# First stage of a hybrid decoder block: norm weights spread by TensorE, ten input slots, another order of loads

## The chip, the cores and the metric

The kernel runs on one core of one Trainium2 chip. The metric is the device time of one execution in microseconds (us). A core has TensorE (PE; its weight loads are listed as PEld), VectorE (DVE), ScalarE (ACT), GpSimd (POOL) and SyncE (SP). Each of them runs its own instructions in program order and waits for the others at semaphores. In this stage SP issues all the DMA transfers.

## What is computed

One decoder block in float32 on x (1024 tokens by 1024 channels) with 256 memory tokens. The first stage computes the three lines below; everything else (gates, state space, forgetting attention, output, cross-attention, FFN) comes after it.

```
u = rms_norm(h, norm_mix[l])
proj = u @ w_in[l]            # the first 512 columns are u_ssm
...
k, v = jnp.split(m @ w_kv, 2, axis=-1)     # m = rms_norm(mem, norm_mem_kv)
```

The state-space branch then needs, for 32 groups of 16 channels with 64 complex states each, lam_bar = exp(lam dt), b_bar = (lam_bar - 1) / lam * b, c and d_skip:

```
bu = jnp.einsum('gpn,blgn->blgp', b_bar, uf)
_, states = lax.associative_scan(...)      # state = lam_bar * state + bu
y = jnp.einsum('gnp,blgp->blgn', c, states).real + d_skip * uf
```

## The kernel before

A float32 product is made of three matmuls on a high and a low part of both operands (`mm3`, L168 to L170: hi*hi, lo*hi, hi*lo). Every operand is split by `split`: ACT casts the high part (L178), then DVE, or POOL where the order says so, subtracts it for the low part (L179). A weight tile is loaded into one of two slots `raw` and split into one of four slots `whi` and `wlo`; a load waits until the tile two before it has been split, and a split waits until the GEMM that used its slot last is through.

**First stage** (`stage_in`). Its work is written as steps, and the table `ORDER_IN` gives their order: F fetches a tile of 128 tokens (m and n are the memory, 0 to 7 are x), G fetches the norm weights, Q, R and S square, take the root and scale a tile (L360, L193 to L203, L217), T turns half a tile by four transposes on PE (L223), E casts and splits the turned half (`uh`, `ul`; `mh`, `ml` for the memory), D loads a weight tile and W splits it (D0 to D7 are the memory's keys and values, D8, D9, Da, Db four blocks of 128 columns of w_in), K and V are the GEMMs of the memory, and U is a GEMM for 128 channels (first digit) and 512 tokens (second digit) with 24 matmuls of 512 columns. X warms PE up. L loads the parameters of the state space (`S5.load`), P are the pieces of `S5.prepare`. A scheduler places the steps' instructions on each engine by the order of the table and by when it believes them ready; a queue then runs as placed. The GEMMs U stand in the order U00 U10 U20 U21 U11 U30 U31 U01, before and after. Where later steps need a slot of `whi`, it is therefore the one of Da's block that comes free first (after U21), then D9's (U11), Db's (U31) and last D8's, after U01, the last GEMM of the stage.

**Parameters.** `S5.load` fetches lam, log_dt, c (in eight transfers), b and d_skip, then turns lam, log_dt and c on PE into `par` and `cT`. `S5.prepare`, all on DVE, makes the powers of lam_bar: exponentials (`exp_parts`, L248 to L257), sine and cosine (`sincos`, L270 to L288, tiles `trg_...`, two of them in the slots that the fetched c leaves), the tables `la` and `ld` (L1205, L1208), and the input coefficients `bb_re`, `bb_im` (L1232 to L1237).

**Second stage** (`stage_ssm`). 32 gate GEMMs of 24 matmuls of 512 columns run on PE. Between them, for each of four quarters q: `weights(q)` on POOL and DVE builds `fre` and `fim` (L1279 to L1282), `Gm` (L1290 to L1298) and the rotations `EC` and `ES` by seven doublings (L1311 to L1313, five on POOL, two on DVE); `turn_weights` turns `fre` and `fim` on PE (L1330) and multiplies them with c (`misc`, L1336), before gate 4 + 7q; `states` reads the stored u (`xg`, L1354), multiplies it with the turned weights (L1361, before gate 5 + 7q) and runs the scan on DVE and POOL (L1369 to L1390); `out` is before gate 9 + 7q. The tiles `fre`, `fim` and their products have one slot each, so `weights(1)` writes `fre` once PE has read the one of quarter 0.

Of the kernel before, what the change touches and what calls it, by code (L numbers as in the profile page):

```python
# [9 lines left out]
F32 = mybir.dt.float32  # L10
# [9 lines left out]
P = 128  # L20
D = 1024
L = 1024
# [16 lines left out]
RSLOT_LATE = (0, 1, 2, 3, 4, 4, 5, 5, 6, 6, 7, 7)  # L39

ORDER_IN = """
G0 Fm Qm Fn D1 X24 Qn Rm D0 Sm F1 G1 Tm0 Rn Em0 Sn Tn0 F0 Tm1 W0 Q0 Tn1 En0 F2 Q1 W1g En1 Em1 K0 D2 F3 K1 R0
S0 T00 T01 k0 E00 Q2 W2g D3 E01 D4 S1 T10 Q3 W3 k1 D5 K3 K2 W4 E10 W5 D6 R1 k2 T11 k3 S2 F4 Q4 V0 F5 S3g T30
E11 D7 Q5 F7 T20 R2 T21 E21 E20 S4 E30 W6 W7 T40 V1 D8 S5 E40 W8 T31 V2 L0 T41 E31 V3 D9 Db T50 F6 Q6 v T51 W9
E51 U00 Da Q7 L1 E41 u00 R3 S6 Wa T60 E50 S7 T61 T70 Wbg E61 U10 E60 P0 U20 u10 T71 E70 E71 u20 P1 U21 U11 U30
P2 u30 U31 u11 u31 U01 u21 P3 P4 P5 u01
"""


# [284 lines left out]
def stage_in(B, xp, s5, x, mem, g_mix, g_kv, w_in, w_mem_kv, uT, u_d, kv_d):  # L334

    V, A, T, S, small = B.V, B.A, B.T, B.S, B.small  # L340
    junk = xp.tile([P, D], BF16, name="junk")
    mT = Act(xp, "mT", 4, 8, ML, kg=4, name="m")
    tiles, gain, ss, rs, raw, w, ps, us, kv = {}, {}, {}, {}, {}, {}, {}, [], []
    names = {"m": -2, "n": -1, **{str(t): t for t in range(NT)}}

    def xtile(name="xt"):
        return xp.tile([P, D], F32, tag="xt", bufs=8, name=name)

    def fetch(t):
        tiles[t] = xtile()  # L350
        S.dma_start(tiles[t], mem[(t + 2) * P:(t + 3) * P, :] if t < 0 else x[t * P:(t + 1) * P, :])

    def gains(i):
        gain[i] = xtile("gain")
        S.dma_start(gain[i], (g_kv if i == 0 else g_mix).partition_broadcast(P))

    def square(t):
        if t % 2 == 0:
            ss[t // 2] = small.tile([P, 2], F32, name="ss2")
        A.activation(junk, tiles[t], AF.Square, scale=1.0 / 32, accum_out=ss[t // 2][:, t % 2:t % 2 + 1])  # L360

    def root(i):
        rs[i] = B.rsqrt(ss[-1][:, i % 2:i % 2 + 1] if i < 0 else ss[i], pool=i < 0)

    def scale(t, pool):
        i = t // 2
        r = rs[t][:, 0:1] if t < 0 else rs[i][:, t % 2:t % 2 + 1]
        B.norm_scale(tiles[t], tiles[t], r, gain[0 if t < 0 else 1], pool=pool)

    def turn(t, b):  # L370
        ps[t, b] = B.turn(tiles[t], b, ("misc", "pv")[b])

    def evac(t, b):
        B.turned(ps.pop((t, b)), b, *((mT, t + 2) if t < 0 else (uT, t)))

    def wget(i):
        if i < 4:
            src = w_mem_kv[:, i * P:(i + 1) * P]
# [5 lines left out]
        S.dma_start(raw[i].rearrange("p (k c) -> p k c", k=D // src.shape[-1]),  # L384
                    src.rearrange("(k p) c -> p k c", p=P))
# [24 lines left out]
    def values(kk):  # L410
        wh, wl = w[4 + kk]
        for t in range(2):
            if kk == 0:
                ps["v", t] = B.bank("sc")
            for k in (2 * kk, 2 * kk + 1):
                B.mm3(ps["v", t], *mT.tok(k, t), wh[:, k % 2, :], wl[:, k % 2, :], k == 0, k == 7)

    def values_out():
        for t in range(2):
            cs = slice(t * 512, (t + 1) * 512)  # L420
            B.split(kv[2][:, cs], kv[3][:, cs], ps.pop(("v", t)))
        for i in range(2, 4):
            S.dma_start(kv_d[i], f32(kv[i]))

    def ssm_in(q, h):
        ps["u", q, h] = B.bank("mm")
        B.gemm_t(ps["u", q, h], *w[8 + q], uT, h, 8)

    def ssm_out(q, h):
        if h == 0:  # L430
            us.append(xp.tile([P, D], F32, tag="kv", bufs=4, name="us"))
        uv = us[q].rearrange("p (t c) -> p t c", t=8)
        A.copy(uv[:, :, 64 * h:64 * h + 64], ps.pop(("u", q, h)).rearrange("p (c t) -> p t c", t=8))
        if h == 1:
            S.dma_start(u_d[q].rearrange("t p c -> p t c"), uv)

    prep = s5.prepare()

    acts = {"F": lambda a: fetch(names[a]), "G": lambda a: gains(int(a)), "Q": lambda a: square(names[a]),
            "R": lambda a: root(names[a]),  # L440
            "S": lambda a: scale(names[a[0]], a[1:] == "g"),
            "T": lambda a: turn(names[a[0]], int(a[1])), "E": lambda a: evac(names[a[0]], int(a[1])),
            "D": lambda a: wget(int(a, 16)), "W": lambda a: wsplit(int(a[0], 16), a[1:] == "g"),
            "K": lambda a: keys(int(a)), "k": lambda a: keys_out(int(a)), "V": lambda a: values(int(a)),
            "v": lambda a: values_out(), "U": lambda a: ssm_in(int(a[0]), int(a[1])),
            "u": lambda a: ssm_out(int(a[0]), int(a[1])), "L": lambda a: s5.load(int(a)),
            "P": lambda a: next(prep, None), "X": lambda a: B.warm(int(a))}
    for step in ORDER_IN.split():
        acts[step[0]](step[1:])
# [661 lines left out]
class S5:  # L1111
# [9 lines left out]
    def load(self, part):  # L1121
# [5 lines left out]
        def pt(name, shape, dt=F32):  # L1127
            return sp.tile([P] + shape, dt, name=name)

        if part == 0:  # L1130
# [4 lines left out]
            S.dma_start(self.ldr[32:48, :], log_dt.rearrange("(j two) -> j two", two=2))  # L1135
            self.craw = []
            for src in (c_re, c_im):
                cr = sp.tile([P, 256], F32, tag="craw", bufs=2, name="craw").rearrange("p (h q) -> p h q", h=2)
                for h in range(2):
                    for two in range(2):  # L1140
                        S.dma_start(cr[:, h, 64 * two:64 * two + 64],
                                    src.rearrange("(j two) m p -> two j m p", two=2)[two, 8 * h:8 * h + 8])
                self.craw.append(cr)
            self.braw = [pt("b_re", [16, 16]), pt("b_im", [16, 16])]
# [3 lines left out]
            S.dma_start(self.dbc, d_skip.partition_broadcast(P))  # L1148
            return
        V.tensor_copy(self.rows[32:48, :].rearrange("j (two p) -> j two p", two=2),  # L1150
                      self.ldr[32:48, :].unsqueeze(2).to_broadcast([16, 2, 64]))
        ps = B.bank("misc")
        T.transpose(ps[:, :48], self.rows, ident[0:48, 0:48])
        self.par = pt("par", [48])
        V.tensor_copy(self.par, ps[:, :48])
        self.cT = [pt("cT_re", [16, 16]), pt("cT_im", [16, 16])]
        for t_, cr in zip(self.cT, self.craw):
            ps = B.bank("misc")
            for h in range(2):
                T.transpose(ps[:, h * P:(h + 1) * P], cr[:, h, :], ident)  # L1160
            V.tensor_copy(t_, ps[:, :256].rearrange("p (j m) -> p j m", j=16))

    def prepare(self):
        B, sp, cT, bb, dbc, par = self.B, self.sp, self.cT, self.braw, self.dbc, self.par
        V, A, G = B.V, B.A, B.G
        lr, li, ld = par[:, 0:16], par[:, 16:32], par[:, 32:48]

# [73 lines left out]
        for i in range(2):  # L1241
            G.memset(self.cb[i], 0.0)
            for g in range(2):
                V.tensor_scalar(out=self.cb[i][64 * g:64 * g + 64, :, g, :], in0=cT[i][64 * g:64 * g + 64],
                                scalar1=1.0 if i == 0 else -1.0, scalar2=None, op0=ALU.mult)

        msk = pt("msk", [16])
# [563 lines left out]
```

## Time and profile before

| | |
|---|---|
| time, median of 3 runs (lowest to highest) | 1593.38 us (1593.16 to 1594.76) |
| time of the profiled execution | 1588.78 us |
| its span, first to last instruction | 1586.7 us |
| PE busy in the span | 1534.0 us (97%) |
| DVE / ACT / POOL busy | 1019.5 / 655.2 / 254.3 us |
| last matmul of the first stage (L170, U01) | 112.06 us, for 0.23 us |
| mean granted clock of PE | 0.988 |

The views that the prediction reads: the page; the chain of waits (what released what, followed back from the last instruction, here cut to the first 200 us: start, duration, what); the windows (length, then busy time and instructions of PE, PEld, DVE, ACT, POOL, then the granted clock, the busy share of the DMA engines and GB/s); the timeline (start, duration, engine, line, operation, output <- inputs, shape, and in brackets the idle time before it and what ended it); and the waits (engine, line <- what it waited for: us in total, times, longest).

### The profile page before, as it was taken

What the parts mean: (1) busy time and instruction counts of PE and PEld (TensorE: products, weight loads), DVE (VectorE), ACT (ScalarE), POOL (GpSimd) and SP (SyncE); (2) the same over time, 40 slices, a digit from 0 to 9 for tenths busy, and PEclk for the clock granted to TensorE, in tenths of its full rate; (3) what the DMA queues carried; (4) which work ended last, traced back from release to release, by engine and by line L of the source; (5) the groups of instructions that cost most, each with busy time, mean ns of one, the idle gap of its engine ahead of it and who ended that gap; (6) DMA issues with size and microseconds to landing.
All of it is one profiled execution on the core that took longest, in us unless ns stands there. A gap on an engine that the chain in (4) does not pass through costs nothing.

```text
span 1586.7 us, 20446 instructions
## 1 busy us (share of the span) xinstructions
PE 1534.0 (97%) x7313; PEld 1261.3 (79%) x7313; DVE 1019.5 (64%) x1850; ACT 655.2 (41%) x1173; POOL 254.3 (16%) x335
## 2 busy tenths in 40 slices
PE   7799999999999899999999999999999999999997
PEld 6578888898777668888888778888888888788885
DVE  6666445344688687675555697766677776565555
ACT  6422434323576553222435564333333333254342
POOL 2027653200212124110002200100000000000001
PEclk8899999999999999999999999999999999999999
DMA  7764445652023736357412186555444554796642
GB/s 266 125 132 80 127 131 110 130 145 30 18 52 48 186 95 208 125 172 259 160 46 75 54 283 239 170 164 163 155 153 160 166 162 156 261 391 223 195 150 106
DMA packets 197940, 240.86 MB, mean 152 GB/s; under 512 B 35448, under 2 KB 126488, under 8 KB 197328
## 3 DMA queue, kind: packets, MB, share of 16 engines
q1 hardware_dynamic: 191216, 223.84, 48.2%
q10 hardware_dynamic: 6624, 15.73, 2.6%
q8 instruction: 57, 0.93, 0.2%
q14 instruction: 43, 0.35, 0.1%
HBM read 165.60 MB, written 75.86 MB: 152 GB/s over the span
## 4 chain that ended last, share of the span: by engine, by line
PE 75%; DVE 8%; DMA 7%; issue 4%; POOL 3%; ACT 2%; SPq 1%; DVEq 0%; POOLq 0%; ACTq 0%
PE mm L868 14%; PE mm L168 7%; PE pv L868 7%; PE mm L170 7%; PE mm L169 7%; PE mm L1005 4%; PE sc L868 3%; PE sc L1005 3%; PE pv L1005 3%; PE sc L168 3%; PE sc L169 3%; PE sc L170 3%; DMA raw<-in_w_in_dram 2%; PE misc L1005 1%; PE pv L168 1%
## 5 line engine op out<-in xcount | busy, mean ns | idle before, releaser
L179 DVE TENSOR_TENSOR wlo<-raw,whi 128x1024 fp32r<-128x1024 f32 (+2 forms) x121 | 132.0, 1094 | 135.1 <-ACT whi L178 133.9
L178 ACT CAST whi<-raw 128x1024 fp32r<-128x1024 f32 (+2 forms) x124 | 116.1, 940 | 220.0 <-DMA raw<-in_w_ffn_in_dram 54.1
L168 PE MATMUL mm<-uh,whi 128*128 128x512 f32 x344 | 138.8, 404 | 2.8 <-ACT whi L178 2.7
L170 PE MATMUL mm<-uh,wlo 128*128 128x512 f32 x344 | 136.5, 397 | 1.7 <-DVE wlo L179 1.7
L169 PE MATMUL mm<-ul,whi 128*128 128x512 f32 x344 | 136.4, 396 | 0.0
L179 DVE TENSOR_TENSOR ol<-or,oh 128x1024 fp32r<-128x1024 f32 x73 | 89.3, 1224 | 71.6 <-ACT oh L178 70.3
L178 ACT CAST oh<-or 128x1024 fp32r<-128x1024 f32 x73 | 76.8, 1052 | 105.3 <-PE mm L1005 33.6
L900 POOL TENSOR_TENSOR g<-a,c 128x512 f32<-128x512 f32 x22 | 35.2, 1600 | 392.8 <-ACT a L899 373.9
L170 PEld LDWEIGHTS mm<-uh,wlo 128*128 128x128 f32 x344 | 65.7, 191 | 16.5 <-DVE wlo L179 3.1
L1630 POOL TENSOR_TENSOR pl<-pf,ph 128x512 fp32r<-128x512 f32 (+1 forms) x32 | 39.7, 1239 | 241.1 <-DVE ph L1629 196.1
L168 PEld LDWEIGHTS mm<-uh,whi 128*128 128x128 f32 x344 | 65.9, 192 | 15.5 <-ACT whi L178 3.2
L169 PEld LDWEIGHTS mm<-ul,whi 128*128 128x128 f32 x344 | 66.0, 192 | 11.3
L197 POOL TENSOR_TENSOR r<-ms,mhalf 128x1 f32<-128x1 f32 x26 | 15.1, 582 | 354.9 <-DVE ms L193 344.5
L1627 ACT ACTIVATE pf<-sc 128x512 f32<-128x512 f32 (+1 forms) x96 | 46.5, 490 | 46.3 <-DVE sc L1623 28.6
L868 PE MATMUL pv<-S3h,we 128*128 128x512 f32 x176 | 58.1, 389 | 0.0
L1633 DVE TENSOR_TENSOR pl<-pf,ph 128x512 fp32r<-128x512 f32 (+2 forms) x64 | 35.1, 550 | 10.2 <-ACT ph L1632 9.5
L1005 PE MATMUL mm<-oh 128*128 128x512 f32 x106 | 41.2, 389 | 0.0
L1005 PE MATMUL mm<-ol,oh 128*128 128x512 f32 x106 | 41.2, 389 | 0.0
L1005 PE MATMUL mm<-oh,ol 128*128 128x512 f32 x106 | 41.2, 389 | 0.0
L168 PE MATMUL mm<-yh,whi 128*128 128x512 f32 x104 | 40.9, 393 | 0.0
L168 PE MATMUL sc<-uh,whi 128*128 128x512 f32 x104 | 40.8, 393 | 0.0
L170 PE MATMUL mm<-yh,wlo 128*128 128x512 f32 x104 | 40.6, 390 | 0.0
(580 smaller groups left out, 4537.5 us busy)
## 6 DMA issues: line engine op xcount, KB each, us to landing
or<-c_d SPq DMA_DIRECT2D x77, 256.0 KB
raw<-in_w_in_dram SPq DMA_DIRECT2D x22, 512.0 KB
wo<-in_w_ffn_out_dram SPq DMA_DIRECT2D x22, 512.0 KB
c_d<-g SPq DMA_DIRECT2D x44, 256.0 KB
t_d<-wo SPq DMA_DIRECT2D x44, 256.0 KB
or<-t_d SPq DMA_DIRECT2D x44, 256.0 KB
raw<-in_w_ffn_in_dram SPq DMA_DIRECT2D x20, 512.0 KB
rawb<-in_w_ffn_in_dram SPq DMA_DIRECT2D x20, 512.0 KB
```

The source lines that it names most:

```text
L168: T.matmul(ps, lh, rh, start=first, stop=False)
L169: T.matmul(ps, lh, rl, start=False, stop=False)
L170: T.matmul(ps, ll, rh, start=False, stop=last)
L178: self.A.copy(hi, src)
L179: (self.G if pool_lo else self.V).tensor_sub(lo, src, f32(hi))
L197: self.G.tensor_tensor(out=r, in0=v, in1=self.mhalf[:, 0:n], op=ALU.pow)
L868: T.matmul(ps, l_[:, k, :], r_, start=first and k == 0 and i == 0, stop=k == 3 and i == 2, skip_group_check=True)
L900: G.tensor_mul(g[:, 512:], a1, c1)
L1005: T.matmul(ps, l_[:, gi], r_[:, 512:], start=n < 3 and p == 0 and k == 0 or n == 7 and p == 0 and k == 0, stop=p == NP - 1 and k == 2, ski ...
L1627: self.exp = A.activation(pf[:, off:], ps[:, off:], AF.Exp)
L1630: G.tensor_sub(pl[:, off:], pf[:, off:], f32(ph[:, off:]))
L1633: V.tensor_sub(pl[:, off:], pf[:, off:], f32(ph[:, off:]))
```

## The change

- **Norm weights.** Before, each of the two gains was fetched by a DMA that spread 1024 values over 128 partitions. Now the two rows are fetched into partitions 0 and 32 of one tile (step g), a tile of ones is set on POOL, and step G spreads each row by two plain float32 matmuls of 512 columns with one contracted row; ACT copies one half out, DVE the other.
- **Slots and order.** The input tiles have ten slots and not eight. Warm-up is 16 + 6 matmuls and not 24. F4 to F7 stand before the loads D4 to D7; F6 and F7 stood behind later ones. D8 and D9 stand ahead of the parameters.
- **Parameters.** `S5.load` has four parts and not two. Part 0 (lam, log_dt, c) follows D9, part 1 (b, d_skip) follows Db, each placed behind the last weight load. Part 2 turns lam and log_dt, part 3, which turns c, stands behind U01 now.
- **c** comes in two transfers of 128 x 4 x 64 and not in eight of 128 x 64, is turned by eight transposes with 64 output rows, and ACT copies it out in four copies where DVE did so in two.
- Wa is split on POOL now, and Wb on DVE; it was the other way round.

```
 ORDER_IN:
-... S5 E40 W8 T31 V2 L0 T41 E31 V3 D9 Db T50 F6 Q6 v T51 W9
-E51 U00 Da Q7 L1 E41 u00 R3 S6 Wa T60 E50 S7 T61 T70 Wbg E61 U10 E60 P0 U20 u10 T71 E70 E71 u20 P1 U21 U11 U30
-P2 u30 U31 u11 u31 U01 u21 P3 P4 P5 u01
+... W7 T40 V1 D8 D9 L0 S5 E40 W8 T31 V2 T41 E31 V3 Da T50 Q6 v T51 W9
+E51 U00 Q7 E41 R3 S6 u00 Db L1 T60 E50 S7 T61 T70 Wag E61 U10 L2 E60 P0 U20 u10 T71 E70 E71 u20 P1 U21 U11 Wb U30
+P2 u30 U31 u11 u31 U01 L3 u21 P3 P4 P5 u01

-        return xp.tile([P, D], F32, tag="xt", bufs=8, name=name)
+        return xp.tile([P, D], F32, tag="xt", bufs=10, name=name)

+    def gain_rows():
+        gain["r"] = xtile("grow")
+        B.G.memset(one, 1.0)
+        for i, g in enumerate((g_kv, g_mix)):
+            S.dma_start(gain["r"][32 * i:32 * i + 1, :], g.rearrange("(o n) -> o n", o=1))
     def gains(i):
         gain[i] = xtile("gain")
-        S.dma_start(gain[i], (g_kv if i == 0 else g_mix).partition_broadcast(P))
+        r = slice(32 * i, 32 * i + 1)
+        for c in range(2):
+            cs = slice(512 * c, 512 * c + 512)
+            ps_ = B.bank("sc")
+            T.matmul(ps_, one[r, :], gain["r"][r, cs], start=True, stop=True)
+            (A.copy, V.tensor_copy)[c](gain[i][:, cs], ps_)

+    def params(i):
+        with B.behind(raw["last"] if i < 2 else None):
+            s5.load(i)

 S5.load, c and its turn:
-                for h in range(2):
-                    for two in range(2):
-                        S.dma_start(cr[:, h, 64 * two:64 * two + 64],
-                                    src.rearrange("(j two) m p -> two j m p", two=2)[two, 8 * h:8 * h + 8])
+                S.dma_start(cr, src.rearrange("(q g) m p -> (g m) q p", q=4))
...
-            for h in range(2):
-                T.transpose(ps[:, h * P:(h + 1) * P], cr[:, h, :], ident)
-            V.tensor_copy(t_, ps[:, :256].rearrange("p (j m) -> p j m", j=16))
+            for q in range(4):
+                T.transpose(ps[0:64, q * P:(q + 1) * P], cr[:, q, :], ident)
+            pv = ps[0:64, :].rearrange("p (j two m) -> p two j m", j=16, two=2)
+            for two in range(2):
+                B.A.copy(t_[64 * two:64 * two + 64], pv[:, two])
```

What this moves on the engines is shown at three places. The lines of `S5` after L1132 are some 18 to 21 higher in the changed program (L1279 is L1300 there, L1232 is L1253, L1311 is L1332).

**SP, the loads of w_in and of the parameters** (`raw<-in_w_in` are D8, D9, Da, Db; `craw` is c, `dbc` is d_skip; `kv_d` stores keys and values). Before:

```order
L384 DMA raw<-in_w_in_dram 128x8x128
L1141 DMA craw<-in_c_re_dram 128x1x64 x3
L1141 DMA craw<-in_c_im_dram 128x1x64 x4
L1146 DMA b_re<-in_b_re_dram 128x16x16
L1146 DMA b_im<-in_b_im_dram 128x16x16
L1148 DMA dbc<-in_d_skip_dram 128x512
L384 DMA raw<-in_w_in_dram 128x8x128 x2
L351 DMA xt<-in_x_dram 128x1024
L423 DMA kv_d<-kv 128x1024 x2
L384 DMA raw<-in_w_in_dram 128x8x128
```

With the change:

```order
L398 DMA raw<-in_w_in_dram 128x8x128 x2
L1150 DMA prow<-in_lam_re_dram 16x128
L1151 DMA prow<-in_lam_im_dram 16x128
L1153 DMA ldr<-in_log_dt_dram 16x2
L1157 DMA craw<-in_c_re_dram 128x4x64
L1157 DMA craw<-in_c_im_dram 128x4x64
L398 DMA raw<-in_w_in_dram 128x8x128
L437 DMA kv_d<-kv 128x1024 x2
L398 DMA raw<-in_w_in_dram 128x8x128
L1163 DMA b_re<-in_b_re_dram 128x16x16
L1163 DMA b_im<-in_b_im_dram 128x16x16
L1165 DMA dbc<-in_d_skip_dram 128x512
```

D9 moved ahead of c, b and d_skip; c stands ahead of Da, and b and d_skip behind Db.

**DVE, the end of the first stage** (`wlo<-raw,whi` are the splits of the first four gate weights; they take the slots of Da's, D9's, Db's and D8's block in this order). Before, two of them stand inside the preparation and two behind its last result:

```order
L1232 TENSOR_TENSOR bb_re<-b_re,qr 128x256
L1227 TENSOR_TENSOR qi<-qi,t_1051 128x16
L1235 TENSOR_TENSOR bb_im<-b_im,qr 128x256
L1228 TENSOR_TENSOR qi<-qi,den 128x16
L1233 TENSOR_TENSOR tb<-b_im,qi 128x256
L1234 TENSOR_TENSOR bb_re<-bb_re,tb 128x256
L1236 TENSOR_TENSOR tb<-b_re,qi 128x256
L1237 TENSOR_TENSOR bb_im<-bb_im,tb 128x256
L179 TENSOR_TENSOR wlo<-raw,whi 128x1024 x2
```

With the change:

```order
L1210 SCALAR_TENSOR_TENSOR R<-ela_p,ela_ib 128x128
L1214 TENSOR_TENSOR e_813<-ela_p,ela_ib 128x16
L1215 TENSOR_TENSOR em<-em,e_813 128x16
L179 TENSOR_TENSOR wlo<-raw,whi 128x1024 x3
L270 TENSOR_SCALAR trg_k<-mt 128x224
L271 TENSOR_SCALAR trg_k<-trg_k 128x224
L179 TENSOR_TENSOR wlo<-raw,whi 128x1024
L272 SCALAR_TENSOR_TENSOR trg_h<-trg_k,mt 128x224
L1265 TENSOR_SCALAR cb_re<-cT_re 64x16x16
```

All four splits stand ahead of the sine and cosine now, and so ahead of `la`, `ld` and `bb`.

**POOL, the start of weights(0).** Before, `fre` is built first, and the doublings of EC and ES follow among the rest:

```order
L179 TENSOR_TENSOR wlo<-raw,whi 128x1024
L1279 TENSOR_TENSOR w_1112<-ld_re,bb_re 128x448
L1280 TENSOR_TENSOR w_1113<-ld_im,bb_im 128x448
L1282 COPY fre<-bb_re 128x4x16
L1282 COPY fim<-bb_im 128x4x16
L1281 TENSOR_TENSOR fre<-w_1112,w_1113 128x4x112
```

With the change, POOL has done all its five doublings when it comes to `fre`:

```order
L1332 TENSOR_TENSOR d_1193<-ES,trg_cs 128x4x16
L1333 TENSOR_TENSOR d_1194<-EC,trg_sn 128x4x16
L1334 TENSOR_TENSOR ES<-d_1193,d_1194 128x4x16
L1300 TENSOR_TENSOR w_1125<-ld_re,bb_re 128x448
L1303 COPY fre<-bb_re 128x4x16
L1301 TENSOR_TENSOR w_1126<-ld_im,bb_im 128x448
L1303 COPY fim<-bb_im 128x4x16
L1302 TENSOR_TENSOR fre<-w_1125,w_1126 128x4x112
```

On DVE the sixth doubling, which reads POOL's last ES, stands ahead of `bb_re` in the changed program. From `weights(1)` on, every engine's instructions stand as before.

More of the change, by code (lines that the diff above doesn't have):

```diff
@@ L341, in stage_in @@
     junk = xp.tile([P, D], BF16, name="junk")
+    one = B.junk.bitcast(F32)[0:33, 0:P]
     mT = Act(xp, "mT", 4, 8, ML, kg=4, name="m")
@@ L383, in wget @@
         raw[i] = B.wpool.tile([P, RAW], F32, tag="raw", bufs=2, name="raw")[:, :D]
-        S.dma_start(raw[i].rearrange("p (k c) -> p k c", k=D // src.shape[-1]),
-                    src.rearrange("(k p) c -> p k c", p=P))
+        raw["last"] = S.dma_start(raw[i].rearrange("p (k c) -> p k c", k=D // src.shape[-1]),
+                                  src.rearrange("(k p) c -> p k c", p=P))
     def wsplit(i, pool):
@@ L435, in ssm_out @@
             S.dma_start(u_d[q].rearrange("t p c -> p t c"), uv)
+    def params(i):
+        with B.behind(raw["last"] if i < 2 else None):
+            s5.load(i)
     prep = s5.prepare()
-    acts = {"F": lambda a: fetch(names[a]), "G": lambda a: gains(int(a)), "Q": lambda a: square(names[a]),
+    acts = {"F": lambda a: fetch(names[a]), "g": lambda a: gain_rows(), "G": lambda a: gains(int(a)), "Q": lambda a: square(names[a]),
             "R": lambda a: root(names[a]),
@@ L445, in stage_in @@
             "v": lambda a: values_out(), "U": lambda a: ssm_in(int(a[0]), int(a[1])),
-            "u": lambda a: ssm_out(int(a[0]), int(a[1])), "L": lambda a: s5.load(int(a)),
+            "u": lambda a: ssm_out(int(a[0]), int(a[1])), "L": lambda a: params(int(a)),
             "P": lambda a: next(prep, None), "X": lambda a: B.warm(int(a))}
@@ L1137, in load @@
             for src in (c_re, c_im):
-                cr = sp.tile([P, 256], F32, tag="craw", bufs=2, name="craw").rearrange("p (h q) -> p h q", h=2)
-                for h in range(2):
-                    for two in range(2):
-                        S.dma_start(cr[:, h, 64 * two:64 * two + 64],
-                                    src.rearrange("(j two) m p -> two j m p", two=2)[two, 8 * h:8 * h + 8])
+                cr = sp.tile([P, 256], F32, tag="craw", bufs=2, name="craw").rearrange("p (q c) -> p q c", q=4)
+                S.dma_start(cr, src.rearrange("(q g) m p -> (g m) q p", q=4))
                 self.craw.append(cr)
+            return
+        if part == 1:
             self.braw = [pt("b_re", [16, 16]), pt("b_im", [16, 16])]
@@ L1149, in load @@
             return
[L1150 to L1155, printed above, removed]
+        if part == 2:
+            V.tensor_copy(self.rows[32:48, :].rearrange("j (two p) -> j two p", two=2),
+                          self.ldr[32:48, :].unsqueeze(2).to_broadcast([16, 2, 64]))
+            ps = B.bank("misc")
+            T.transpose(ps[:, :48], self.rows, ident[0:48, 0:48])
+            self.par = pt("par", [48])
+            V.tensor_copy(self.par, ps[:, :48])
+            return
         self.cT = [pt("cT_re", [16, 16]), pt("cT_im", [16, 16])]
@@ L1243, in prepare @@
             for g in range(2):
-                V.tensor_scalar(out=self.cb[i][64 * g:64 * g + 64, :, g, :], in0=cT[i][64 * g:64 * g + 64],
+                V.tensor_scalar(out=self.cb[i][64 * g:64 * g + 64, :, g, :], in0=self.cT[i][64 * g:64 * g + 64],
                                 scalar1=1.0 if i == 0 else -1.0, scalar2=None, op0=ALU.mult)
```

8 lines of the change are left out of this document (4 added, 4 removed).

## The prediction

> **What bounds the kernel now.** I read the page first: is any engine full?
>
> ```profile
> span 1586.7 us, 20446 instructions
> PE   7799999999999899999999999999999999999997
> ```
>
> PE is full nearly everywhere. Each slice is 39.7 us; the lean ones at the front (7, 7) are the first stage, the only place that the change touches. The second view is the chain of waits, followed forward from the start.
>
> ```profile
> 23.80 4.46 DMA raw<-in_w_mem_kv_dram
> ...
> 38.84 9.74 DMA raw<-in_w_in_dram
> ...
> 51.76 8.97 DMA raw<-in_w_in_dram
> ...
> 64.70 8.15 DMA raw<-in_w_in_dram
> 72.88 2.01 ACT whi L178
> ...
> 76.81 1.19 DVE xt L217
> 78.00 0.66 DVE ul L179 x2
> ...
> 112.06 0.23 PE mm L170
> ...
> 136.55 1.16 POOL fre L1281
> ...
> 179.20 10.61 DMA xg<-u_d
> 189.94 2.02 PE pv L1361 x16
> ```
>
> Three blocks of w_in in a row (D8, D9, Da) set the end of the first stage, 112.06 + 0.23 = 112.3. The later rows say what takes over: POOL's `fre`, a store and a read of u, and `states(1)` at 189.94. The third view is the windows, for PE and its clock.
>
> ```profile
> 30.00:40.00 10.00, 8.87 (x56) 7.66 (x56) 9.96 (x26) 7.21 (x17) 2.41 (x1) 1.00 0.64 225
> 50.00:52.00 2.00, 0.00 (x0) 0.00 (x0) 1.39 (x1) 0.85 (x2) 0.00 (x0) 1.00 0.77 79
> 54.00:56.00 2.00, 2.00 (x10) 1.90 (x10) 1.85 (x4) 1.40 (x5) 0.00 (x0) 0.50 1.09 84
> 190.00:200.00 10.00, 10.00 (x52) 8.56 (x53) 7.83 (x10) 3.66 (x10) 4.54 (x3) 1.00 0.55 139
> ```
>
> At 50 to 52 PE does nothing while it waits for a block of w_in; from 30 to 40 DVE is busy 9.96 of 10 us, so there no load is the limit. The fourth view, the waits from 110 to 420 us, has one entry on the way to `states(1)`:
>
> ```profile
> PE pv L1361 <- DMA xg<-u_d: 1.6, 1, 1.6
> ```
>
> So between 112 and 190 us PE has 1.6 us of slack against the chain on POOL, DVE and SP that makes `fre(1)` and then u's read. Behind `states(1)` nothing of this stage is waited for again, and the instructions there stand in the same order in both programs. **What the change is worth is therefore when PE passes `states(1)`:** how much earlier the first stage ends, less how much later that chain runs against its end.
>
> **Part 1: norm weights.** Two DMAs of 512 KB as written go; four plain float32 matmuls of 512 columns and four copies come, before the memory's first GEMM.
>
> ```profile
> 142.04 1.95 PE L1361 MATMUL pv<-xg,F 128*128 128x128 f32 x16
> ```
>
> Sixteen records here are eight plain products of 128 columns: 1.95 / 8 = 0.24 each, so about 1 us for 512 columns and 4 us for four at full clock, 8 at half. They fall where PE otherwise warms up and waits for the memory's weights (the load at 23.80 is one), and up to 40 us DVE is the limit. The cover is gone if the rows arrive late: then the warm-up and the memory's GEMMs, queued behind these matmuls on PE, start late. Bounds: 2 us gained (an earlier transfer) to 4 lost. I take **0**, since the 30 to 40 row is the nearest. The ten slots and the earlier F4 to F7 are taken at 0 with it, for the same row: the tiles are not late there, DVE is.
>
> **Part 2: loads.** The queue of SP, in its timeline before:
>
> ```profile
> 39.27 4.72 SPq L1141 DMA_DIRECT2D craw<-in_c_re_dram  x3
> 44.04 3.58 SPq L1141 DMA_DIRECT2D craw<-in_c_im_dram  x4
> 50.67 0.98 SPq L1148 DMA_DIRECT2D dbc<-in_d_skip_dram  x1
> ```
>
> D9 was issued at 51.76, after these. Now it needs only W7's split, some 43 us, an estimate from D8's issue at 38.84 by one tile of 4 us. D8 itself goes out some 1.5 us later (a scaling, 1.19, stands ahead of W6 on DVE). At 8 to 9.7 us a load D8 is in by 49 to 50, at 4.5 (the memory's row at 23.80) by 45. W8 is split behind the x work on DVE, about 48.5, and only then is Da asked for, with c ahead of it in the queue. Its landing: 48.5 + 4.5 = 53 to 48.5 + 8.2 + four of queue = 61. I take **55.5**, nearer the short end, because two blocks and not three are then under way.
>
> From Da's landing on, DVE and ACT lead. Wa's two casts (2.01 in the chain) stand on ACT ahead of the casts of `uh` that DVE's `ul` (0.66 for two) and then the scaling of x tile 6 (1.19) wait for; with a cast of `uh` (under 0.5, an estimate from `ul`, which is as large) about 4.3 us. Then U10 follows, 5.4 by the next rows, with its transposes: about 10 us behind Da's landing, and six GEMMs more.
>
> ```profile
> 106.70 1.05 ACT L178 CAST whi<-raw 128x1024 fp32r<-128x1024 f32 x1 [4.67 <-PE mm L169]
> 112.10 1.05 ACT L178 CAST whi<-raw 128x1024 fp32r<-128x1024 f32 x1 [3.86 <-PE mm L169]
> ```
>
> The casts of the gate weights follow U31 and U01, 5.40 apart: with transposes 33 us for six. The stage ends at 55.5 + 10 + 33 = about **99** (96 to 104 with Da's bounds), which is **13.3 us earlier**. (Before, 64.70 + 8.15 + 39.5 = 112.3; the 3.5 more are tile 6, then already scaled.)
>
> **Part 3: the chain.** On DVE the gate weights' fourth split now stands ahead of sine and cosine, and c is turned by PE behind U01. Both wait for the end of the stage. On DVE's timeline before:
>
> ```profile
> 88.53 0.26 DVE L277 TENSOR_SCALAR trg_s<-trg_h 128x224 f32<-128x224 f32 x1
> ...
> 94.42 0.27 DVE L1205 TENSOR_TENSOR la_im<-R,trg_sn 128x128 f32<-128x128 f32 x1
> ...
> 98.58 0.42 DVE L1232 TENSOR_TENSOR bb_re<-b_re,qr 128x256 f32<-128x256 f32 x1
> ...
> 100.00 0.42 DVE L1234 TENSOR_TENSOR bb_re<-bb_re,tb 128x256 f32<-128x256 f32 x1
> ...
> 113.18 1.23 DVE L179 TENSOR_TENSOR wlo<-raw,whi 128x1024 fp32r<-128x1024 f32 x1 [4.17 <-ACT whi L178]
> ```
>
> Sine and cosine were done by 94.7 and `bb_re` by 100.4, well before the stage's end at 112.3; nothing waited for them. Now, counted from the stage's end: the split 113.18 + 1.23 - 112.3 = 2.1; the five steps L272 to L276, 0.26 to 0.38 each like L277, with DVE's part of waiting for c's copies, taken as 2.2 (1.5 without); L277 to L1205 94.42 - 88.53 = 5.9 less the 1.2 of a split inside it, 4.7. The angles are there at **+9.0**. POOL takes them next; its timeline:
>
> ```profile
> 100.50 1.24 POOL L1279 TENSOR_TENSOR w<-ld_re,bb_re 128x448 f32<-128x448 f32 x1 [19.74 <-DVE bb_re L1234]
> ...
> 103.47 1.16 POOL L1281 TENSOR_TENSOR fre<-w,w 128x448 f32<-128x448 f32 x1
> ...
> 132.54 1.00 POOL L1279 TENSOR_TENSOR w<-ld_re,bb_re 128x448 f32<-128x448 f32 x1
> 133.50 1.04 POOL L1280 TENSOR_TENSOR w<-ld_im,bb_im 128x448 f32<-128x448 f32 x1
> 136.55 1.16 POOL L1281 TENSOR_TENSOR fre<-w,w 128x448 f32<-128x448 f32 x1 [2.02 <-PE misc L1336]
> ...
> 142.97 1.97 POOL L1290 TENSOR_TENSOR w<-la_re,cT_re 128x512 f32<-128x512 f32 x1
> ...
> 148.63 1.10 POOL L1291 TENSOR_TENSOR w<-la_im,cT_re 128x512 f32<-128x512 f32 x1
> ...
> 160.71 0.62 POOL L1311 TENSOR_TENSOR d<-EC,trg_cs 128x4 f32<-128x4 f32 x1
> ...
> 170.32 0.32 POOL L1313 TENSOR_TENSOR ES<-d,d 128x64 f32<-128x64 f32 x1
> ```
>
> POOL's five doublings of the rotations now stand ahead of `fre(0)`: 170.64 - 160.71 = 9.9 (8 without its slow rows), to +18.9. DVE's two further doublings wait for POOL's last and stand ahead of the last steps of `bb`: 100.42 - 98.58 = 1.8 and 0.6, +21.3. Then POOL's `fre(0)`, 104.63 - 100.50 = 4.1, +25.4; `fim(0)`, three such products, 3.2, +28.6; Gm, 149.73 - 142.97 = 6.8, +35.4; its last sum on DVE hidden by the next two products (1.00, 1.04) and a little waiting, `fre(1)` at +38.2. Before it was at 136.55 - 112.3 = +24.2. So the chain is **14.0 us later** against the stage's end (12.5 to 15.6). PE finds it out in steps: at `turn_weights(0)`, which it would reach at about +22, some 6 us for `fim`; at `out(0)`, 3 to 5; the rest at `states(1)`. What lies between `fre(1)` and `states(1)`, 189.94 - 136.55 = 53.4 us, is unchanged.
>
> **c in two transfers** frees SP of some 6 us in rows of 39.27 and 44.04, which is in Da's 55.5; its eight transposes and ACT's four copies are in the 2.2. **Wa on POOL, Wb on DVE**: Wb has U20 to U11 as cover, 0.
>
> **Sum.** -13.3 + 14.0 + 0 = **+0.7**. Against the profiled execution, 1588.78, that is 1589.5. The median, 1593.38, lies 4.6 above it, and the verdict is against it: 1593.4 + 0.7 = **1594**.
>
> A point beside the sum: does a last stall cost more than itself? In the windows the clock is 0.50 at 54 to 56, behind the empty 50 to 52, and 1.00 at 190 to 200, behind the stall of 1.6. The Trainium skill, "TensorE: Matmul & The Clock Gate", section "Part 1: The HAM clock gate (the "warmup" mystery)", has the clock halve after an idle window of about 3.4 us and return after as long a busy one. By that rule, and this trace agrees as far as these rows go, each stall over 3.4 us is followed by 3.4 at half speed, 1.7 lost (an estimate from that page). The time ahead of `states(1)` is the chain's, so only a stall at that place adds: the sum would be +2.4 by the rule, where that stall is so long, and +0.7 by the 190 to 200 row.
>
> **Rivals.**
> *The loads come quicker.* At 4.5 us a block (row at 23.80) Da lands at 52.5, the stage ends at 95.5, 16.8 earlier, and with POOL's doublings at 8 us and little else in them the chain is 12.5 late: -4.3, **1589**. For it: the DMA share is only 0.64 at 30 to 40 and 0.77 at 50 to 52. Against: all three rows of w_in say 8 to 9.7.
> *The loads stay slow (slower).* Place: Da, behind c and beside D9, b and d_skip. At 8 us and more it lands at 61, the stage ends at 104, 8.3 earlier, and the chain takes 14.0: +5.7, **1599**. It decides from Da's landing at 58.5 on (stage end 101.5, +3.2). For it: the three rows. Against: before, each of them stood behind other transfers.
> *The chain is not what PE waits for.* If the fourth split doesn't hold DVE (it is ready early, or POOL and DVE take the steps in other stretches of slack), only the stage's 13.3 is left: **1580**. For it: 1.6 us is the only wait there now. Against: an engine runs its queue in order, and the split needs U01's slot.
>
> **How the numbers follow.** The two shifts cancel: 48%, 1594, own range 1589.6 (-16.8 + 13) to 1597. Quicker loads 16%; slow loads 28%; no chain 8%. What a measurement of this kernel can tell from no change is about 0.2%, 3.2 us. Of the 48, 42 lie within, 2 below, 4 above: faster 2 + 16 + 8 = 0.26, same 0.42, slower 4 + 28 = 0.32. The range: below, 1589 less up to 2 for the gains, 1587; above, -8.3 + 15 = +6.7, 1600. Left out are the 1580 and the edges.
>
> **What would show it.** Da's landing at 55 (52 to 61) and the last matmul of U01 near 99; DVE's split behind U01 ahead of sine and cosine; POOL's first doubling 9 us behind the stage's end; waits of PE on `fim` and on u's read between 115 and 190; `states(1)` near 190 again. Wrong if PE has no such waits, if `states(1)` moves by over 5 us, or if anything behind it waits newly.

## The result and the profile after

| | before | changed |
|---|---|---|
| median, four runs each | 1593.27 us | 1607.32 us (1602.60 to 1608.61) |
| ratio to before (95% interval) | | 1.0086 (1.0069 to 1.0104) |
| profiled execution, its span | 1588.78, 1586.7 us | 1608.00, 1606.3 us |
| last matmul of the first stage ends | 112.3 us | 114.1 us |
| `states(1)` starts | 189.94 us | 205.32 us |

The changed kernel is slower by 0.86%, 13.7 us of 1593 (11.0 to 16.6). The forecast was 1594, with a range of 1587 to 1600; the time lies above it. The page has the same shape as before, with the lean slices in other places:

```profile
span 1606.3 us, 20464 instructions
PE   8698989999999999999999999999999999999997
```

The waits of PE in the first 300 us, where the kernel before had 1.6 us behind the first stage:

```profile
PE misc L223 <- DVE ul L179: 10.1, 2, 8.2
...
PE pv L1382 <- DMA xg<-u_d: 4.2, 1, 4.2
PE pv L223 <- DVE xt L217: 2.7, 1, 2.7
PE pv L1351 <- POOL fre L1302: 2.7, 1, 2.7
PE pv L1351 <- POOL fim L1302: 2.5, 1, 2.5
```

The prediction had named the waits on `fim` and on `xg`. The one on `fre` stands beside that on `fim`, together 5.2 us at `turn_weights(0)` where 6 had been forecast; the wait of 3 to 5 us at `out(0)` did not come (0.3 there). The waits on `ul` and `xt` (10.1 and 2.7) are in the first stage. The chain of waits, cut to the first 230 us, tells what became of the earlier loads:

```profile
44.26 10.57 DMA raw<-in_w_in_dram
...
54.86 1.91 ACT whi L178
...
65.01 7.13 SPq L1163
72.19 6.10 DMA dbc<-in_d_skip_dram
78.31 0.69 DVE dbc L1273
79.00 0.35 DVE ul L179
...
113.88 0.23 PE mm L170
114.11 0.45 PE misc L1179 x4
114.58 0.29 DVE trg_k L270
...
115.09 1.22 DVE wlo L179
...
194.64 10.55 DMA xg<-u_d
205.32 3.75 PE pv L1382 x16
```

D8 is asked for at 44.26 (before 38.84, forecast 40.3) and lands at 54.8 (forecast 49 to 50). D9, asked for next, is no longer in the chain, so that part of the change works; in its place stand d_skip, which SP could issue only after 7.13 us in the issue of b (before 1.62), and DVE's masking of it. The stage ends at 114.1, where 99 had been forecast.

The rows at 114.11 and 114.58 show what starts the other chain late. `trg_k`, the first tile of sine and cosine, takes a slot that the fetched c leaves, so DVE's first step waits for PE's turn of c, which now stands behind the last GEMM of the stage. The split of a gate weight at 115.09 comes after that.

The chain's own steps on POOL, in its timeline:

```profile
123.85 0.30 POOL L1333 TENSOR_TENSOR d<-ES,trg_sn 128x4 f32<-128x4 f32 x1 [2.78 <-DVE trg_sn L286]
...
131.89 0.32 POOL L1334 TENSOR_TENSOR ES<-d,d 128x64 f32<-128x64 f32 x1
...
138.16 1.39 POOL L1302 TENSOR_TENSOR fre<-w,w 128x448 f32<-128x448 f32 x1
...
141.88 1.19 POOL L1302 TENSOR_TENSOR fim<-w,w 128x448 f32<-128x448 f32 x1
...
154.59 1.13 POOL L1302 TENSOR_TENSOR fre<-w,w 128x448 f32<-128x448 f32 x1
```

Against the stage's end, 114.1: first doubling +9.7 (forecast +9.0), last +18.1 (+18.9), `fre(0)` done +25.4 (+25.4), `fim(0)` +29.0 (+28.6), `fre(1)` +40.5 (+38.2). That half of the prediction held step by step; the other half did not.

From the stage's end to `states(1)` it is 13.6 us more than before. PE's waits there are 7.8 us more (2.7, 2.5 and 4.2 against 1.6). Most of the rest is the clock: it is 0.50 from 140 to 150 us, behind the waits on `fre` and `fim`, and PE is busy for 7.5 of these 10 us, so about 3.8 us are lost (an estimate from these two numbers). PE then still waits 4.2 us for `xg`.

### The profile page after: what moved, and what is told of

The parts are those of the page before. It is cut to its first block, busy times and chain, and to the rows that moved or that the text cites. A ratio compares the mean times of both kernels' runs of the same rounds, so it can differ in the third digit from the quotient of the medians.

```text
span 1606.3 us, 20464 instructions
## 1 busy us (share of the span) xinstructions
PE 1549.5 (96%) x7323; PEld 1272.1 (79%) x7323; DVE 1025.3 (64%) x1850; ACT 657.7 (41%) x1179; POOL 252.8 (16%) x336
## 4 chain that ended last, share of the span: by engine, by line
PE 79%; DVE 6%; DMA 5%; issue 4%; POOL 3%; ACT 2%; SPq 1%; DVEq 0%; POOLq 0%; ACTq 0%
PE mm L886 15%; PE pv L886 7%; PE mm L168 7%; PE mm L170 7%; PE mm L169 7%; PE mm L1023 5%; PE sc L886 4%; PE sc L1023 4%; PE pv L1023 3%; PE sc L168 3%; PE sc L170 3%; PE sc L169 3%; PE misc L1023 2%; DMA raw<-in_w_in_dram 2%; PE pv L168 1%
## 5 line engine op out<-in xcount | busy, mean ns | idle before, releaser
L197 POOL TENSOR_TENSOR r<-ms,mhalf 128x1 f32<-128x1 f32 x26 | 16.1, 621 | 353.2 <-DVE ms L193 344.0
L170 PE MATMUL sc<-uh,wlo 128*128 128x512 f32 x104 | 41.0, 395 | 0.0
L169 PE MATMUL sc<-ul,whi 128*128 128x512 f32 x104 | 41.0, 394 | 0.0
```

What stands on the lines that cost most here:

```text
L169: T.matmul(ps, lh, rl, start=False, stop=False)
L170: T.matmul(ps, ll, rh, start=False, stop=last)
L197: self.G.tensor_tensor(out=r, in0=v, in1=self.mhalf[:, 0:n], op=ALU.pow)
```

## The experiments

The kernels were run in three sets (e1, e2, e3 and e6; e5 and e7 to e9; e10 to e12), each in five rounds beside the kernel before on a chip of its own; a ratio is always to the kernel before on that chip. The stage's end in this section is the start of ACT's cast that waits for U01, since it has one row in every kernel:

| kernel | stage's end | `states(1)` | between | ratio to before (95% interval) |
|---|---|---|---|---|
| before | 112.10 | 189.94 | 77.8 | |
| changed | 113.92 | 205.32 | 91.4 | 1.0086 (1.0069 to 1.0104) |
| e1, c turned early | 114.11 | 192.17 | 78.1 | 1.0000 (0.9988 to 1.0012) |
| e2, before with c turned late | 113.54 | 205.98 | 92.4 | 1.0101 (1.0084 to 1.0118) |
| e3, gains by DMA | 110.86 | 202.27 | 91.4 | 1.0076 (1.0059 to 1.0093) |
| e5, e1 and e3 together | 111.28 | 189.66 | 78.4 | 1.0002 (0.9991 to 1.0013) |
| e6, before with TensorE's gains | 115.95 | 194.66 | 78.7 | 1.0008 (0.9997 to 1.0018) |
| e7, load order alone | 110.75 | 188.42 | 77.7 | 0.9988 (0.9976 to 0.9999) |
| e8, e5 with b ahead of Db | 115.77 | 194.20 | 78.4 | 1.0031 (1.0019 to 1.0042) |
| e9, e5 with Wa on DVE | 110.81 | 189.04 | 78.2 | 1.0001 (0.9991 to 1.0011) |
| e10, e7 with b late, Wa on DVE | 113.83 | 191.12 | 77.3 | 0.9999 (0.9986 to 1.0012) |
| e11, own slots for D8, D9 | 110.35 | 187.98 | 77.6 | 0.9988 (0.9973 to 1.0003) |
| e12, e11 with D8 later | 109.97 | 186.89 | 76.9 | 0.9997 (0.9987 to 1.0008) |

The column "between" falls into two groups: 77 to 79 where c is turned early, 91 to 93 where it is turned behind U01. One profiled execution is not exact at the front: e1 has the changed kernel's instructions up to D8, and asked for it at 46.17, not 44.26. So single ends are good to some 2 us, and the ratios decide.

**e1: c turned early.**

```
-... E61 U10 L2 E60 ... u31 U01 L3 u21 P3 P4 P5 u01
+... E61 U10 L2 L3 E60 ... u31 U01 u21 P3 P4 P5 u01
```

Expected:

> The changed kernel with one step moved: the turn of c (L3) stands behind L2 again and not behind U01. Theory A, the price is the chain (the changed kernel's first fre(1) stood 40.5 us behind the first stage's end, before 24.2): sine and cosine run inside the first stage again, fre(1) falls back to some 24 us behind its end, states(1) from 205.3 to about 192, PE's waits on fre, fim and xg (2.7, 2.5, 4.2) are gone, and the time is 1593.3 plus the 1.8 us by which the first stage ends later: 1595 (1592 to 1598). Theory B, the price is paid in the first stage and by its transfers, and the chain only fills slack: the time stays within 4 us of the changed kernel, 1603 to 1609.

The changed kernel's PE timeline at `states(1)`, then that of e1, where the number in brackets is the wait ahead of it:

```profile
205.32 3.75 PE L1382 MATMUL pv<-xg,F 128*128 128x128 f32 x16 [4.15 <-DMA xg<-u_d]
```

```profile
192.17 2.02 PE L1382 MATMUL pv<-xg,F 128*128 128x128 f32 x16 [1.77 <-DMA xg<-u_d]
```

Moving one step takes the whole loss away: ratio 1.0000, and the wait is 1.77 as it was 1.6 before. Theory A holds. The rest of the change together is worth nothing, within 0.12% either way.

**e2: the kernel before with that step alone.**

```
+        if part == 1:
             ...              # lam and log_dt are turned, as before
+            return
         self.cT = [...]      # c is turned, as before
-... u11 u31 U01 u21 P3 P4 P5 u01
+... u11 u31 U01 L2 u21 P3 P4 P5 u01
```

> The kernel before with one part of the change alone: c is turned behind U01 (its loads, its copies on DVE and all else as before). Theory A (chain): the first stage ends at about 112.3 as before, sine and cosine and POOL's doublings come behind it, fre(1) some 38 to 41 us behind its end, states(1) 12 to 16 us later, and with a little half-clock time behind the stall 1606 to 1611. Theory B: 1592 to 1596, as the chain finds cover.

```profile
205.98 3.76 PE L1363 MATMUL pv<-xg,F 128*128 128x128 f32 x16 [4.48 <-DMA xg<-u_d]
```

1609.0, slower by 1.01%, 16.1 us (13.4 to 18.8), with all loads as before. The chain's price is shown from both sides: 13.7 us taken away in e1, 16.1 added in e2; forecast 14.0. In e2 the fourth gate split stands on DVE at 118.21, behind seven of the steps of sine and cosine and not ahead of them, and "between" is 92.4 all the same: it is the turn of c that holds the chain, not the split.

**e3 and e6: the norm weights.** e3 is the changed kernel with the first line of the table and the gains as before; e6 is the kernel before with those of the change, and with its ten input slots:

```
-G0 Fm Qm Fn D1 X24 Qn Rm D0 Sm F1 G1 Tm0 ...
+Fm g Fn X16 D0 G0 X6 Qm Qn Rm D1 Sm F1 Tm0 ... Q0 G1 Tn1 ...
```

> The changed kernel with the norm weights spread by DMA as before (first line of the table and the gains as before, all else as changed). Theory A2, the plain float32 matmuls hold up the front: D8 was asked for at 44.26 in the changed kernel and at 38.84 before; here it is asked for by 39 to 41, the first stage ends 4 to 6 us before 114.1, and the time is 1601 to 1604, with the chain's price left. Theory B2, the front is paced by the x tiles and the memory's weights whichever way the gains come: D8 after 43, time 1605 to 1609.

> The kernel before with one part of the change alone: the norm weights spread by TensorE, with the warm-up split and ten input slots. Theory A2: D8 is asked for 4 to 6 us later than at 38.84, the first stage ends as much later, 116 to 118, and the time is 1597 to 1600. Theory B2 (the forecast's 0): D8 within 1.5 us of 38.84, time 1591 to 1596.

In e6 SP's timeline has D8 4 us later than the 38.84 of before:

```profile
42.79 0.38 SPq L398 DMA_DIRECT2D raw<-in_w_in_dram  x1
```

The mechanism of theory A2 is there: D8 4 us later and the stage's end 3.9 later in e6, 3.1 earlier in e3 without it. The price is small, and the times that theory A2 gave (1597 to 1600 for e6) did not come: e6 is slower by 1.3 us (-0.5 to 2.9), which lies where theory B2 had it, and e1, with TensorE's gains, is no slower than e5, without them (1.0000 and 1.0002, on two chips). Zero is not excluded; the profiled execution of e6, 1597.15, was the slowest of its twelve. In e3, without TensorE's gains, D8 was asked for at 42.81, so they are not the only thing that delays it.

**e5, e7: what the load order is worth.** e5 undoes the chain and the gains. e7 puts the x tiles back too, so that the order of the loads is left, with c in two transfers and the exchange of Wa and Wb. The edit of e7 against e5:

```
-... E01 F4 F5 D4 S1 ... W5 F7 D6 R1 F6 k2 ... Q4 V0 S3g ... D7 Q5 T20 ... Da T50 Q6
+... E01 D4 S1 ... W5 D6 R1 k2 ... F4 Q4 V0 F5 S3g ... D7 Q5 F7 T20 ... Da T50 F6 Q6
-        return xp.tile([P, D], F32, tag="xt", bufs=10, name=name)
+        return xp.tile([P, D], F32, tag="xt", bufs=8, name=name)
```

> The changed kernel with both costs undone: c turned behind L2, norm weights spread by DMA; ten slots, the x tiles' and weights' earlier loads and c in two transfers stay. If chain and front add, as the single runs say (first stage's end 110.9 with the gains by DMA, states(1) 78 us behind it with c early): states(1) at 188 to 190, time 0.997 to 1.001 of before, 1588 to 1594. If the early loads do bring what was forecast (13 us) once nothing holds them up: 1579 to 1583.

> The run above with the x tiles F4 to F7 fetched where they were before, in eight slots: what is left of the change is D9 ahead of the parameters, Db and Da exchanged with them, c in two transfers. Theory C, the earlier squares and scalings of x tiles 4 to 7 hold up the memory's last splits on ACT and DVE (D8 was asked for at 42.8 with them and without TensorE's gains, at 38.84 before): D8 at 39 to 40.5, the first stage's end 107 to 109, time 1588 to 1591. Theory D, D8 waits for the memory's weights themselves: D8 at 42 to 43, end 110 to 112, time as the run above.

Theory C holds for D8, which e7 asks for at 38.92, and in e7's ACT timeline the cast of Da's block (the third) waits for nothing, 13 us before its time in the kernel before:

```profile
48.32 1.91 ACT L178 CAST whi<-raw 128x1024 fp32r<-128x1024 f32 x1 [4.29 <-DMA raw<-in_w_in_dram]
52.49 1.99 ACT L178 CAST whi<-raw 128x1024 fp32r<-128x1024 f32 x1
59.38 2.00 ACT L178 CAST whi<-raw 128x1024 fp32r<-128x1024 f32 x1
68.70 1.97 ACT L178 CAST whi<-raw 128x1024 fp32r<-128x1024 f32 x1 [1.63 <-DMA raw<-in_w_in_dram]
...
110.75 1.05 ACT L178 CAST whi<-raw 128x1024 fp32r<-128x1024 f32 x1 [3.86 <-PE mm L169]
```

But the stage ends only 1.4 us earlier, where theory C had 3 to 5, and the time is better by 1.9 us (0.2 to 3.8). Where the 13 us went, PE's waits from 47 to 112 us of e7 tell:

```profile
PE misc L223 <- DVE ul L179: 6.3, 2, 4.7
PE misc L223 <- DVE xt L217: 2.3, 1, 2.3
```

With 0.4 for the turn of the parameters, 9.0 us, where the kernel before had 10.7 in the same stretch: the earlier block is followed at once by other waits. Their causes stand in e7's DVE timeline:

```profile
62.36 2.01 DVE L203 SCALAR_TENSOR_TENSOR r<-rt,r 128x2 f32<-128x2 f32 x1
64.29 0.41 DVE L179 TENSOR_TENSOR ul<-misc,uh 128x256 fp32r<-128x256 f32 x1
64.62 2.46 DVE L217 SCALAR_TENSOR_TENSOR xt<-xt,r,gain 128x1024 f32<-128x1024 f32 x2
67.11 0.42 DVE L179 TENSOR_TENSOR ul<-misc,uh 128x256 fp32r<-128x256 f32 x1
70.70 1.94 DVE L179 TENSOR_TENSOR wlo<-raw,whi 128x1024 fp32r<-128x1024 f32 x1 [3.17 <-ACT whi L178]
...
74.25 0.69 DVE L1259 TENSOR_TENSOR dbc<-dbc,msk 128x512 f32<-128x512 f32 x1 [0.94 <-DMA dbc<-in_d_skip_dram]
```

A root of two columns takes 2.01 us beside POOL's split of Wa (61.46, 2.89 us); then DVE waits 3.17 for the cast of Wb, which waits for Db; then for d_skip. In an in-order queue each of them holds the `ul` behind it, which PE needs.

**e8, e9, e10: taking those waits away.**

```
 e8   -u00 Db L1 T60            +u00 L1 Db T60
 e9   -Wag ... U11 Wb U30       +Wa ... U11 Wbg U30
 e10  -Db L1 T60 ... E60 P0 U20 u10 T71 E70 E71 u20
      +Db T60 ... E60 U20 u10 T71 E70 E71 L1 P0 u20    (and as e9)
```

> The first run of this set with b and d_skip asked for ahead of Db and not behind it. In the changed kernel d_skip landed at 78.3, and its masking stood on DVE ahead of a split of u for which PE waited 1.9 us. Theory E, that hold is part of why the first stage does not end earlier: d_skip lands by 72, the wait goes, and the stage ends 2 to 4 us earlier. Theory F, PE is held there by the scaling of tiles 6 and 7 and by Wa: the end moves by less than 1 us either way, and Db, now later, is not waited for.

> The first run of this set with Wa split on DVE and Wb on POOL, as before the change. In the changed kernel two small DVE operations beside POOL's split of Wa took 2.0 us and not 0.17, and PE waited 2.7 us for the scaling behind them. Theory G, POOL's split slows DVE at the place that PE waits for: on DVE the split is over sooner (1.9 us), and the stage ends 1 to 3 us earlier. Theory H, the split of Wa stands ahead of that scaling on DVE then, with the same length: end within 1 us.

> The load order alone (run e7, in which Da landed 13 us before its time in the kernel before and the stage still ended only 1.4 us earlier), with the two things for which PE waited there behind Da taken away: Wa split on DVE and Wb on POOL as before, and b, d_skip and the first pieces of the preparation behind the last turn of x. Theory I, waits that come up in the place of Da's eat the gain: without POOL's split of Wa beside it the scaling of tiles 6 and 7 is 2 us sooner (PE waited 2.3), without d_skip's masking 1.6 more; the stage ends at 106 to 109 and the time is 1587 to 1590. Theory J, PE's own work from the first U on sets the end, with what it cannot start sooner: end at 110 to 111.5, time within 1.5 us of the run e7.

e8 is slower by 0.31%, 4.9 us (3.0 to 6.7): d_skip was masked at 70.17, but Db came later, and ACT waited for it, with a cast of u that PE needs queued behind. Theory F falls, since Db is waited for. Theory E is not tested by it: in e5, from which it starts, PE has no wait behind the masking (74.88), and in e8, where the masking came 4.7 us earlier, PE waited 1.88 us for the `ul` behind it. Its ACT timeline:

```profile
76.12 1.94 ACT L178 CAST whi<-raw 128x1024 fp32r<-128x1024 f32 x1 [6.47 <-DMA raw<-in_w_in_dram]
```

e9 waits 9.7 us for `ul`, and e5, from which it starts, 9.6: the end moves by 0.5 us, as theory H had it. But e5 has no slow root and no wait for the scaling, so this pair doesn't test theory G. e10 does: its roots take 0.15 to 0.18 us and the masking comes at 76.78, where PE does not wait behind it, yet PE still waits 9.8 us in that stretch, 3.79 of it at 75 behind a cast of a late Db. It ended the stage at 113.83, in a profiled execution of 1596.74 that was the slowest of its twelve; its ratio, 0.9999, is no better than that of e7 either. No edit of the three shortened the stage by more than 0.5 us, so theory I did not hold.

**e11, e12: the loads asked for much earlier.**

```
+        raw[i] = (xp.tile([P, D], F32, tag="raw8", bufs=2, name="raw") if i in (8, 9) else ...
-... D6 R1 ... E11 D7 Q5 ... W6 W7 T40 V1 D8 D9 L0 S5 ... V3 Da T50 ... u00 Db L1 T60
+... D6 D8 R1 ... E11 D7 D9 Q5 ... W6 Da W7 Db L0 T40 V1 S5 ... V3 T50 ... u00 L1 T60
```

e12 has D8 behind D7 in the table and D9 behind E21. Both start from e7 and split Wa on DVE and Wb on POOL.

> As e7, but D8 and D9 are loaded into two slots of their own, so that they and then Da and Db are asked for some 10 us sooner (D8 ahead of D4, D9 ahead of D6, Da behind W6); Wa on DVE, Wb on POOL. Theory K, the loads of w_in bound the stage by when they are asked for: PE's wait ahead of the first U (4.6 us before, 4.7 in e7) goes, and the stage ends 3 to 6 us earlier than in e7, 105 to 108, time 1585 to 1589. Theory J, DVE, which is busy 9.9 of 10 us from 30 to 40, and PE bound it: the end moves by under 2 us, and D8's transfer ahead of the memory's weights holds those up.

> As e11, with D8 only ahead of D6 and D9 ahead of D7, so that fewer of the memory's weights wait behind them. Theory K: as e11 or 1 to 2 us better, end 104 to 107. Theory J: end 109 to 111.

D8 is asked for at 17.9 and 26.9 instead of 38.9. The stage ends at 110.35 and 109.97, against 110.75 in e7, and the times are 0.9988 (0.9973 to 1.0003) and 0.9997. Theory K, that the stage ends when the loads of w_in let it, falls. In e12's windows, the engines that PE waits for are full, one after the other:

```profile
40.00:50.00 10.00, 5.20 (x21) 4.38 (x22) 7.09 (x18) 4.67 (x11) 0.00 (x0) 0.83 0.94 260
50.00:60.00 10.00, 9.59 (x51) 7.78 (x50) 8.70 (x15) 10.00 (x15) 0.00 (x0) 1.00 0.88 140
60.00:70.00 10.00, 4.57 (x21) 3.71 (x20) 9.16 (x14) 3.74 (x7) 2.85 (x1) 0.92 0.95 197
```

From 40 to 50 the transfers are at 0.94, and the memory's last block, asked for at 39.9 behind D9 (before at 37.7), is still on its way; from 50 to 60 ACT is busy 10.00 of 10 us with the casts of weights, of u and of the memory and the squares of two x tiles that have come together there; from 60 to 70 DVE is busy 9.16. PE's waits are 5.4 us on the scaling and 4.9 on a root. Which of them would have to give way for the stage to end before 110 was not settled.

## Why the prediction was wrong

**Right: what bounds the kernel.** The time goes by when PE passes `states(1)`. Over the eleven experiments `states(1)` moved by -3 to +16 us, and the times follow it to within 3.4 us (e6: +4.7 and +1.3).

**Right: the chain (part 3), with one of its two causes.** 14.0 us was forecast, 13.7 and 16.1 us were measured (e1, e2). It had put both the fourth split and the turn of c in front of sine and cosine; the turn of c alone does it (e2). Where it came out later than forecast, by 2.3 at `fre(1)`, POOL waited 1.56 us a second time for DVE's Gm, and two products beside DVE took 1.97 and not 1.0. It was given back before `states(1)`: 50.7 us between the two, and not 53.4.

**Wrong: the end of the first stage (part 2), forecast 13.3 us earlier and measured 1.8 later.** Two steps of its sum failed. The first is "W8 is split behind the x work on DVE, about 48.5, and only then is Da asked for". Measured:

- D8 was asked for at 44.26, not 40.3. TensorE's gains hold it up by 4.0 us in e6 (42.79), the earlier x tiles by 3.3 (42.18 in e5, 38.92 in e7); part 1 had taken both at 0.
- Its load took 10.57 us, where 8 to 9.7 had been taken from the three rows of w_in. The short end, 4.46, was the row of a block of the memory's weights, two rows of 512 columns per partition and not eight of 128.
- Cast and split, 1.91 and 1.89 us, lie between D8's landing and W8's end. The same paragraph put D8 in "by 49 to 50" and W8's end at 48.5, so it contradicted itself: by its own rows Da could not be asked for before 53.

Da was asked for at 58.72 and was there at 65.7 (forecast 55.5; the slow rival said 61). The 7.0 us between are those of the forecast, 48.5 to 55.5: the request was late, not the transfer. Da's landing and the forecast's 10 + 33 then give 108.7, and the stage ended 5.4 later still, of which PE waited 2.7 for the scaling and 1.9 behind d_skip: waits that the sum did not have.

**The second step that failed is the 10 + 33 us behind Da's landing.** In e7 Da is there by 59.4 and the stage ends at 110.75, 51 behind it; in the kernel before it was 39.5. In e11 Da came ahead of the forecast's 55.5: its cast, the second of these two in ACT's timeline, is over at 54.94.

```profile
51.05 3.89 ACT L178 CAST whi<-raw 128x1024 fp32r<-128x1024 f32 x2
```

The stage still ended at 110.35, not at 99. So the stage does not end a fixed time behind Da, and an earlier request alone would not have brought the 13.3 us. Da was the last of a row of waits before, and its landing did not set the end alone. A bound that needs no wait at all would have shown it: the first U cannot get past its second matmul before W8's split, 53.3 by the forecast's own landing (49.5 + 1.9 + 1.9), and eight GEMMs of 5.40 are 43.2, so the stage cannot end before 96.5 plus its transposes. The forecast of 99 had left 2.5 us for transposes and waits together, where the trace of before has 10.7 us of waits alone.

**The rival that came nearest** was the slow one: same sign, same place, from Da's landing past 58.5. Its price, +5.7, was too low, since it still had the stage end 8.3 us earlier. Had the prediction taken 0 for the first stage, as e1 shows it, its sum would have been +14.0, and 13.7 was measured.

**The clock at `states(1)`** was weighed beside the sum at 1.7 us for a stall over 3.4. The stall was 4.2. In the changed kernel's timeline PE's matmuls took 0.63 where they take 0.39 until 211.4, six microseconds behind the restart, so about 3 us were lost (an estimate from these rows). With the 15.4 at `states(1)` that makes 18.4 of the 19.2 by which the two profiled executions differ. The medians differ by 14.0 only, since the profiled execution of the kernel before was 4.5 us faster than its median; how much of the 3 us is in the medians was not separated.

**Two versions stand level with or just ahead of the kernel before:** the load order alone (e7), 0.9988 (0.9976 to 0.9999), and with slots of its own for D8 and D9 (e11), 0.9988 (0.9973 to 1.0003). Both are below what was called measurable, 0.2%.

## What to carry to other kernels

Where an edit frees a wait in a stage with in-order queues, add up the bounding engine's own work from its first possible start to the end, and put the waits of the trace on top: what the wait is worth is what that sum leaves, and other waits take its place. A chain of dependent small steps was predicted well here by adding the rows step by step. A step that frees a slot belongs to the chain of whoever writes that slot next, and put behind the last GEMM of a stage it costs the next stage its head start. Take a transfer's time from a row of the same shape and the same place, and don't leave out the cast and the split that stand between its landing and the next request.

## What the runs showed of the hardware that was not expected

**The clock can fall after a stall of about 2 us.** `states(1)` is the same sixteen records in every kernel, behind a different stall each time. The PE timelines of e9, e5 and e6:

```profile
189.04 2.02 PE L1368 MATMUL pv<-xg,F 128*128 128x128 f32 x16 [1.98 <-DMA xg<-u_d]
```

```profile
189.66 2.67 PE L1368 MATMUL pv<-xg,F 128*128 128x128 f32 x16 [2.12 <-DMA xg<-u_d]
```

```profile
194.66 3.52 PE L1375 MATMUL pv<-xg,F 128*128 128x128 f32 x16 [2.42 <-DMA xg<-u_d]
```

With waits of up to 1.98 us (seven kernels) they take 2.02; behind 2.12 (e5; e8 with 2.14 alike) 2.67, behind 2.42 3.52, and behind 4.13 to 4.48 they take 3.60 to 3.76. The Trainium skill, "TensorE: Matmul & The Clock Gate", section "Part 1: The HAM clock gate (the "warmup" mystery)", puts the fall behind an idle window of about 3.4 us and says that the window runs freely. At this place 2.1 us was enough, so the measurement decides; the half rate lasted from 3.4 us (e3) to 6 us (the changed kernel). Elsewhere the length of a stall does not settle it. Two rows of PE's timeline in e10:

```profile
44.67 0.74 PE L223 MATMUL misc<-ident,xt 128*128 128x128 f32 x4 [1.88 <-DVE ul L179]
...
60.49 0.63 PE L223 MATMUL misc<-ident,xt 128*128 128x128 f32 x4 [2.87 <-DVE ul L179]
```

Behind the shorter stall the clock is 0.50 (46 to 48 us), behind the longer one 1.00 (62 to 64 us). What decides between 1.9 and 2.9 us was not tried; no stall of that length is safe.

**A tiny DVE operation can be held until POOL's ends.** `r` of two columns took 2.01 us beside POOL's split in e7 and ended with it (64.37 and 64.35); where POOL was idle it took 0.16 (e9). The Trainium skill, "SBUF — State Buffer", section "SBUF: two separate sides", has the two engines share a pair of ports that one holds for a whole instruction; the row agrees, though the stage ended no earlier where the split did not stand beside the root (e10).

**The issue of one transfer can hold SP.** That of b's second half took 7.13 us in the changed kernel behind Db, and 1.62 before. What it waited for there was not tried.
